# Moving one row of each partition to short transfers at the two ends of a DMA-fed softmax

## The chip, the core and the metric

The kernel runs on one core of a Trainium2 chip. The metric is the device time of one execution in microseconds (us): the median of several runs. A profile is one further execution with the hardware profiler on; its span runs from the first to the last instruction that it records.

## The reference

The input `logits` has the shape (2, 8, 2112, 2112) in float32, `rel_bias` (8, 33). For each batch, head and query row the kernel adds a bias that depends on the clipped distance of query and key, and takes a softmax over the 2112 keys:

```python
rel = pos[:, None] - pos[None, :]
bias = rel_bias[:, np.clip(rel, -16, 16) + 16]
logits = logits + bias[None]
e = np.exp(logits - logits.max(axis=-1, keepdims=True))
out = e / e.sum(axis=-1, keepdims=True)
```

So 285 MB are read, 285 MB are written, and each row of 2112 numbers (8448 bytes) is worked on by itself.

## The kernel before

There are 2 x 8 x 2112 rows. Each of the 128 partitions owns 264 consecutive ones (`ROWS`), so partitions 0 to 63 hold the first batch and 64 to 127 the second. A tile is 6 rows of every partition (`R`), one contiguous stretch of 50,688 bytes per partition in memory, 6.5 MB in all. Four buffers `X[0]` to `X[3]` hold tiles; 44 tiles go through them in turn, and each is changed in place and stored from where it was loaded.

**SP issues every large DMA.** First the 6 rows of tile 0 by one DMA each (line 88), then tiles 1 to 3 whole (line 78). Then it stores tile 0 (line 82, called from line 203) and enters its loop (lines 204 to 208). There, for each buffer in turn, it waits until the next tile has been scaled, issues that tile's store, waits until the store of the buffer before has landed (`st[b]`), and issues the load of a new tile into that buffer. After the loop come the stores of the last three tiles, the very last in two halves of 3 rows, and the waits for the stores. An instruction of SP that waits holds up all that SP would issue after it.

**ACT** issues one small DMA for `rel_bias` (line 97) and afterwards computes: for each row an exponential with its sum (line 175). **DVE** builds the table `M` of biases in PSUM (lines 118 to 155). Then it loops over 11 steps of 24 rows: `strip` copies the piece of `M` that this step needs into `F` (line 160); `add` waits for a buffer's load (`ld[b]`), and adds bias and finds the row maximum, one instruction per row (line 166); `scale` takes reciprocals of the sums (line 183) and multiplies the rows (line 187), three at a time. DVE works in program order: the six adds of a tile, then its six multiplications. **POOL** makes two small index tables (lines 101, 102) and is idle from then on.

The order of all this is written out by hand, with semaphores: `pre` and `ld` for loads, `st` for stores, `added`, `expd`, `inv` and `scaled` between DVE, ACT and SP. `take` waits for a semaphore and lowers it again. The waits appear in the profile under line 74.

Of the kernel before, what the change touches and what calls it, by code (L numbers as in the profile page):

```python
# [7 lines left out]
FP32 = mybir.dt.float32  # L8
I32 = mybir.dt.int32
EXP = mybir.ActivationFunctionType.Exp  # L10
ALU = mybir.AluOpType
# [4 lines left out]
def kernel(  # L16
# [21 lines left out]
    MW = S + ROWS - 1  # L38
    FW = S + STEP - 1
    BIG = 3.0e38  # L40

    io = ctx.enter_context(tc.tile_pool(name="io", bufs=1))
# [6 lines left out]
    ip = io.tile([P, 3, PB], I32, tag="ip", name="ip")  # L49
    ps = ctx.enter_context(tc.tile_pool(name="ps", bufs=1, space=bass.MemoryType.PSUM))  # L50
    M = ps.tile([P, 4096], FP32, tag="M", name="M")

    def view(t, offset, dims):

        return bass.AP(tensor=t.tensor, offset=t.offset + offset, ap=[[list(t.ap[0])[0], P]] + dims)

    def rows(t, j, n):

        return bass.AP(tensor=t.tensor, offset=t.offset + j * S, ap=[[ROWS * S, P], [1, n * S]])

    with tc.tile_critical(no_gpsimd_drain=True):
        ld = [nc.alloc_semaphore(f"ld{b}") for b in range(NBUF)]
# [8 lines left out]
        dve = nc.alloc_semaphore("dve")  # L71

        def take(eng, sem, n):
            eng.wait_ge(sem, n).then_inc(sem, -n)  # L74

        def load(j, b):
            nc.sync.dma_start(out=X[b][:, :], in_=rows(logits, j, R)).then_inc(ld[b], 16)

        def store(j, b, s0=0, n=R):  # L80
            take(nc.sync, scaled, n)
            nc.sync.dma_start(
                out=rows(out, j + s0, n), in_=X[b][:, s0 * S : (s0 + n) * S]
            ).then_inc(st[b], 16)

        for r in range(R):
            nc.sync.dma_start(
                out=X[0][:, r * S : (r + 1) * S], in_=rows(logits, r, 1)
            ).then_inc(ld[0] if r == R - 1 else pre, 16)  # L90
        for n in range(1, NBUF):
            load(n * R, n)

# [8 lines left out]
        nc.gpsimd.iota(ip[:, 2], pattern=[[1, PB]], base=0, channel_multiplier=0).then_inc(idx, 1)  # L102

        v = nc.vector
        done = [0]
# [5 lines left out]
        def settle():  # L111
# [7 lines left out]
                             op0=ALU.logical_shift_right, op1=ALU.bitwise_and))  # L119
# [7 lines left out]
        for m, op in ((eq, ALU.is_equal), (gt, ALU.is_gt), (le, ALU.is_le), (lt, ALU.is_lt)):  # L127
# [4 lines left out]
            out=view(F, 0, [[W, H], [1, W]]), in0=view(F, 0, [[W, H], [1, W]]),  # L132
            in1=view(F, SC + 3 * PB, [[1, H], [0, W]]), op=ALU.mult))
# [8 lines left out]
            out=view(F, 0, [[W, PB], [1, W]]), in0=view(F, SC + 2 * PB, [[1, PB], [0, W]]),  # L142
            in1=view(rbS, W - 1, [[0, PB], [-1, W]]), op=ALU.mult))
# [6 lines left out]
            out=view(M, U, [[ROWS, PB], [1, W]]), in0=view(F, 0, [[W, PB], [1, W]]),  # L150
            in1=view(F, SC + 8 * PB, [[1, PB], [0, W]]), op=ALU.add))
        then(v.tensor_copy(out=view(M, U + W, [[ROWS, PB], [1, ROWS - W]]),  # L152
                           in_=view(F, SC + 7 * PB, [[1, PB], [0, ROWS - W]])))
# [4 lines left out]
        def strip(j):  # L158

            v.tensor_copy(out=F[:, :], in_=M[:, bass.ds(ROWS - STEP - j, FW)]).then_inc(dve, 1)  # L160

        def add(b):
            take(v, ld[b], 16)
            for r in range(b * R, (b + 1) * R):
                x = X[b][:, (r - b * R) * S : (r - b * R + 1) * S]
                v.tensor_tensor_reduce(  # L166
                    out=x, in0=x, in1=F[:, STEP - 1 - r : STEP - 1 - r + S], scale=-1.0, scalar=BIG,
                    op0=ALU.add, op1=ALU.min, accum_out=nmax[:, r : r + 1],
                ).then_inc(added, 1)

        def exps(b):
            for r in range(b * R, (b + 1) * R):
                x = X[b][:, (r - b * R) * S : (r - b * R + 1) * S]
                take(nc.scalar, added, 1)
                nc.scalar.activation(  # L175
                    out=x, in_=x, func=EXP, scale=-1.0, bias=nmax[:, r : r + 1],
                    accum_out=tot[:, r : r + 1],
                ).then_inc(expd, 1)

        def scale(b):  # L180
            for r0 in range(b * R, (b + 1) * R, HALF):
                take(v, expd, HALF)
                v.reciprocal(out=rec[:, r0 : r0 + HALF], in_=tot[:, r0 : r0 + HALF]).then_inc(inv, 1)  # L183
                take(v, inv, 1)
                for r in range(r0, r0 + HALF):
                    x = X[b][:, (r - b * R) * S : (r - b * R + 1) * S]
                    v.tensor_scalar_mul(out=x, in0=x, scalar1=rec[:, r : r + 1]).then_inc(scaled, 1)  # L187

        v.sem_inc(dve, -done[0])
        take(v, pre, 16 * (R - 1))  # L190
        with nc.Fori(0, ROWS - STEP + 1, STEP, engines=[ENG.DVE]) as j:  # L191
            strip(j)
            take(v, dve, 1)
            for b in range(NBUF):
                add(b)
                scale(b)
        with nc.Fori(0, ROWS // STEP, 1, engines=[ENG.Activation]):
# [14 lines left out]
        store((N - 1) * R, (N - 1) % NBUF, HALF, R - HALF)  # L212
        for b in range(NBUF):
            take(nc.sync, st[b], 32 if b == (N - 1) % NBUF else 16)

# [28 lines left out]
```

## Time and profile before

| | us |
|---|---|
| median of 3 runs | 1331.23 |
| lowest, highest run | 1330.0, 1331.38 |
| span of the profiled execution | 1327.7 |
| median less span (what lies around the span) | 3.5 |
| DVE busy | 976.6 |
| ACT busy | 575.2 |
| POOL busy | 0.4 |

For the profiled execution the span is what is known of its time, so the 3.5 us between it and the median are taken for what lies around a span. The profile also records the packets of the core's 16 DMA engines: when each started, how long it took, how many bytes it carried, and on which queue. SP's DMAs are queue q1, ACT's are q10. A packet's engine number isn't recorded. In tables of windows the DMA share and the rate count a packet where it starts, so in windows of a few us a share can pass 1.

### The profile page before, as it was taken

To read this page: it belongs to the slowest core of one execution; us is meant where nothing else is said; L and a number is where in the kernel's file an instruction comes from. 1 tells how busy PE (TensorE), PEld (TensorE's weight loads), DVE (VectorE), ACT (ScalarE), POOL (GpSimd) and SP (SyncE) were. 2 spreads that over 40 slices of the span, in tenths; PEclk is the share of its full clock that TensorE was granted. 3 is DMA by queue.
4 is the path that set the end of the run, shared out by engine and by line. 5 is a ranking of instruction groups with operands and counts; after the bars stand their busy time and mean duration, and the time that the engine had idled before them with its cause. 6 is when DMAs were issued, how large, how long until landed. Compare 5 with 4: busy or idle time off the path is not lost. (4 is left out here: it accounts for less than half of the span.)

```text
span 1327.7 us, 2454 instructions
## 1 busy us (share of the span) xinstructions
DVE 976.6 (74%) x911; ACT 575.2 (43%) x539; POOL 0.4 (0%) x6
## 2 busy tenths in 40 slices
DVE  6999667777777776687778777677877776687772
ACT  2564333444444343345444333444444343335440
POOL 0000000000000000000000000000000000000000
DMA  9999999999999999999999999999999999999998
GB/s 392 431 428 437 435 420 437 435 434 425 435 437 434 428 435 434 435 429 429 438 438 432 426 438 437 437 425 437 437 437 425 435 440 437 428 432 438 437 426 359
DMA packets 13683, 571.11 MB, mean 430 GB/s; under 512 B 1521, under 2 KB 1649, under 8 KB 1649
## 3 DMA queue, kind: packets, MB, share of 16 engines
q1 hardware_dynamic: 13536, 570.96, 99.6%
q10 hardware_dynamic: 144, 0.14, 0.1%
q14 instruction: 3, 0.02, 0.0%
HBM read 285.61 MB, written 285.47 MB: 430 GB/s over the span
## 5 line engine op out<-in xcount | busy, mean ns | idle before, releaser
L166 DVE CUSTOM_DVE_ANT_0 X<-X,F 128x2112 f32<-128x2112 f32 x264 | 605.2, 2354 | 301.3 <-DVEq L74 301.3
L175 ACT ACTIVATE X<-X,nmax 128x2112 f32<-128x2112 f32 x264 | 541.7, 2052 | 539.3 <-ACTq L74 517.6
L187 DVE TENSOR_SCALAR X<-X,rec 128x2112 f32<-128x2112 f32 x264 | 332.4, 1315 | 13.2
L175 ACT ACT_TABLE_LOAD x11 | 14.1, 1283 | 183.3 <-ACTq L74 183.3
L175 ACT ACTIVATION_READ_ACCUMULATOR X<-X,nmax 128x1 f32 x264 | 49.2, 186 | 0.0
L160 DVE COPY F<-M 128x2135 f32 x11 | 26.1, 2374 | 6.3 <-DVEq L74 6.3
L166 DVE DVE_READ_ACCUMULATOR2_ANT nmax<- 128x1 f32 x264 | 21.7, 82 | 0.0
L183 DVE RECIPROCAL rec<-tot 128x3 f32<-128x3 f32 x88 | 14.9, 170 | 0.0
L131 DVE TENSOR_TENSOR F<-F 128x264 f32<-128x264 f32 x1 | 0.4, 434 | 4.7 <-DMA F<-in_rel_bias_dram 4.7
L152 DVE COPY M<-F 128x1848 f32<-128x1848 f32 x1 | 2.1, 2077 | 0.0
L118 DVE TENSOR_SCALAR ip<-ip 128x8 int32<-128x8 int32 x1 | 0.2, 173 | 1.3 <-POOL ip L102 1.3
L135 DVE TENSOR_REDUCE rbS<-F 128x33 f32<-128x264 f32 x1 | 0.6, 610 | 0.0
L149 DVE TENSOR_TENSOR M<-F 128x264 f32<-128x264 f32 x1 | 0.4, 441 | 0.0
L141 DVE TENSOR_TENSOR F<-F,rbS 128x264 f32<-128x264 f32 x1 | 0.4, 425 | 0.0
L128 DVE TENSOR_SCALAR F<-F 128x8 f32<-128x8 f32 x4 | 0.4, 166 | 0.0
L154 DVE COPY M<-rbS 128x247 f32<-128x247 f32 x1 | 0.4, 408 | 0.0
L139 DVE TENSOR_SCALAR F<-F,rbS 128x8 f32<-128x8 f32 x1 | 0.2, 231 | 0.0
L145 DVE SCALAR_TENSOR_TENSOR F<-F,rbS 128x8 f32<-128x8 f32 x1 | 0.2, 225 | 0.0
L140 DVE TENSOR_SCALAR F<-F,rbS 128x8 f32<-128x8 f32 x1 | 0.2, 222 | 0.0
L146 DVE SCALAR_TENSOR_TENSOR F<-F,rbS 128x8 f32<-128x8 f32 x1 | 0.2, 219 | 0.0
L124 DVE TENSOR_TENSOR F<-ip 128x8 f32<-128x8 int32 x1 | 0.2, 167 | 0.0
L121 DVE TENSOR_TENSOR F<-ip 128x8 f32<-128x8 int32 x1 | 0.2, 166 | 0.0
(9 smaller groups left out, 1.2 us busy)
## 6 DMA issues: line engine op xcount, KB each, us to landing
X<-in_logits_dram SPq DMA_DIRECT2D x43, 6336.0 KB, 44.6
out_dram<-X SPq DMA_DIRECT2D x43, 6336.0 KB, 52.6
X<-in_logits_dram SPq DMA_DIRECT2D x6, 1056.0 KB, 12.1
out_dram<-X SPq DMA_DIRECT2D x2, 3168.0 KB, 21.1
F<-in_rel_bias_dram ACTq DMA_DIRECT2D x1, 132.0 KB, 6.2
```

Source lines behind the costliest of these rows:

```text
L128: then(v.tensor_scalar(out=m, in0=dp, scalar1=0.0, scalar2=None, op0=op))
L131: then(v.tensor_tensor(out=view(F, 0, [[W, H], [1, W]]), in0=view(F, 0, [[W, H], [1, W]]), in1=view(F, SC + 3 * PB, [[1, H], [0, W]]), op= ...
L135: then(v.tensor_reduce(out=rbS[:, :], in_=view(F, 0, [[1, W], [W, H]]), axis=mybir.AxisListType.X, op=ALU.add))
L141: then(v.tensor_tensor(out=view(F, 0, [[W, PB], [1, W]]), in0=view(F, SC + 2 * PB, [[1, PB], [0, W]]), in1=view(rbS, W - 1, [[0, PB], [-1, ...
L149: then(v.tensor_tensor(out=view(M, U, [[ROWS, PB], [1, W]]), in0=view(F, 0, [[W, PB], [1, W]]), in1=view(F, SC + 8 * PB, [[1, PB], [0, W]] ...
L152: then(v.tensor_copy(out=view(M, U + W, [[ROWS, PB], [1, ROWS - W]]), in_=view(F, SC + 7 * PB, [[1, PB], [0, ROWS - W]])))
L154: then(v.tensor_copy(out=M[:, 0:U], in_=low.to_broadcast([P, U])))
L160: v.tensor_copy(out=F[:, :], in_=M[:, bass.ds(ROWS - STEP - j, FW)]).then_inc(dve, 1)
L166: v.tensor_tensor_reduce(out=x, in0=x, in1=F[:, STEP - 1 - r : STEP - 1 - r + S], scale=-1.0, scalar=BIG, op0=ALU.add, op1=ALU.min, accum_ ...
L175: nc.scalar.activation(out=x, in_=x, func=EXP, scale=-1.0, bias=nmax[:, r : r + 1], accum_out=tot[:, r : r + 1],).then_inc(expd, 1)
L183: v.reciprocal(out=rec[:, r0 : r0 + HALF], in_=tot[:, r0 : r0 + HALF]).then_inc(inv, 1)
L187: v.tensor_scalar_mul(out=x, in0=x, scalar1=rec[:, r : r + 1]).then_inc(scaled, 1)
```

## The change

One row (number 5, `XR`) of each partition leaves the tiles. In tile 0, SP loads and stores rows 0 to 4 alone. The rest goes by transfers of 8 partitions each, eight of them for 64 partitions (`few` names the 8 rows in memory, `fewx` the place in `X[0]`; the 8 partitions of a transfer lie 4 apart):

- **Row 5 of partitions 64 to 127** is loaded and stored by POOL. POOL clears row 5 of the lower 64 partitions in `X[0]`, resets the cursor by which its transfers choose DMA engines, and issues eight pairs: a transfer of 8 single numbers into the scratch tile `pad` (`skip`, meant to take up engines 0 to 7), and 8 rows of logits (meant for engines 8 to 15). It then waits for `told`, and issues eight such pairs again, this time with 8 rows stored to `out`. Semaphore `hx[i]` counts the eight row transfers, `sk[i]` the skips.
- **DVE** waits ahead of its loop for the clearing and for all eight `hx`, and computes all six rows of tile 0 as before (in the lower half of row 5, on zeros that are never stored).
- **SP** stores rows 0 to 4 of tile 0, raises `told`, and waits until all eight `hx` show 32, that is, until POOL's stores have landed. Only then it enters its loop.
- **Row 5 of partitions 0 to 63** is loaded after SP's loop into row 0 of `X[0]`, by eight DMAs of SP, once the last store from `X[0]` has landed. DVE, ACT and DVE work on it after the last tile (add, exponential, reciprocal, multiplication on 64 partitions), and SP stores it by eight DMAs, its last.

```diff
-        for r in range(R):
+        def few(t, half, i, r):
+            p = half * HP + (i // 4) * 32 + i % 4
+            return bass.AP(tensor=t.tensor, offset=t.offset + (p * ROWS + r) * S, ap=[[4 * ROWS * S, 8], [1, S]])
...
+        def skip(i, c):
+            w = list(pad.ap[0])[0]
+            nc.gpsimd.dma_start(
+                out=bass.AP(tensor=pad.tensor, offset=pad.offset + c, ap=[[w, 8], [1, 1]]),
+                in_=bass.AP(tensor=rel_bias.tensor, offset=rel_bias.offset, ap=[[W, 8], [1, 1]]),
+            ).then_inc(sk[i], 16)
+
+        for r in range(XR):
             nc.sync.dma_start(
                 out=X[0][:, r * S : (r + 1) * S], in_=rows(logits, r, 1)
-            ).then_inc(ld[0] if r == R - 1 else pre, 16)
+            ).then_inc(ld[0] if r == XR - 1 else pre, 16)
...
+        g = nc.gpsimd
+        g.memset(X[0][0:HP, XR * S : R * S], 0.0).then_inc(zero, 1)
+        g.inc_swdge_sem([], values=[], queue_num=0, mode="reset_dge_cursor")
+        for i in range(EX):
+            skip(i, i)
+            g.dma_start(out=fewx(1, i, XR), in_=few(logits, 1, i, XR)).then_inc(hx[i], 16)
+        g.wait_ge(told, 1)
+        for i in range(EX):
+            g.wait_ge(sk[i], 16)
+            g.wait_ge(hx[i], 16)
+            skip(i, EX + i)
+            g.dma_start(out=few(out, 1, i, XR), in_=fewx(1, i, XR)).then_inc(hx[i], 16)
...
-        take(v, pre, 16 * (R - 1))
+        take(v, pre, 16 * (XR - 1))
+        v.wait_ge(zero, 1)
+        for i in range(EX):
+            v.wait_ge(hx[i], 16)
         with nc.Fori(0, ROWS - STEP + 1, STEP, engines=[ENG.DVE]) as j:
...
+        xx = X[0][0:HP, 0:S]
+        take(v, xl, 16 * EX)
+        v.tensor_tensor_reduce(out=xx, in0=xx, in1=M[0:HP, ROWS - 1 - XR : ROWS - 1 - XR + S], ...)
+        take(v, expd, 1)
+        v.reciprocal(out=rec[0:HP, 0:1], in_=tot[0:HP, 0:1]).then_inc(inv, 1)
+        take(v, inv, 1)
+        v.tensor_scalar_mul(out=xx, in0=xx, scalar1=rec[0:HP, 0:1]).then_inc(scaled, 1)
...
-        store(0, 0)
+        take(nc.sync, scaled, R)
+        nc.sync.dma_start(out=rows(out, 0, XR), in_=X[0][:, 0 : XR * S]).then_inc(st[0], 16)
+        nc.sync.sem_inc(told, 1)
+        for i in range(EX):
+            nc.sync.wait_ge(hx[i], 32)
         with nc.Fori(0, ROWS - 2 * STEP + 1, STEP, engines=[ENG.SP]) as j:
...
+        take(nc.sync, st[0], 16)
+        for i in range(EX):
+            nc.sync.dma_start(out=fewx(0, i, 0), in_=few(logits, 0, i, XR)).then_inc(xl, 16)
         for n in range(N - NBUF + 1, N - 1):
             store(n * R, n % NBUF)
...
+        take(nc.sync, scaled, 1)
+        for i in range(EX):
+            nc.sync.dma_start(out=few(out, 0, i, XR), in_=fewx(0, i, 0)).then_inc(xs, 16)
```

More of the change, by code (lines that the diff above doesn't have):

```diff
@@ L40 @@
     BIG = 3.0e38
+    XR = R - 1
+    HP = P // 2
+    EX = 8
     io = ctx.enter_context(tc.tile_pool(name="io", bufs=1))
@@ L49 @@
     ip = io.tile([P, 3, PB], I32, tag="ip", name="ip")
+    pad = io.tile([P, 2 * EX], FP32, tag="pad", name="pad")
     ps = ctx.enter_context(tc.tile_pool(name="ps", bufs=1, space=bass.MemoryType.PSUM))
@@ L71 @@
         dve = nc.alloc_semaphore("dve")
+        zero = nc.alloc_semaphore("zero")
+        told = nc.alloc_semaphore("told")
+        xl = nc.alloc_semaphore("xl")
+        xs = nc.alloc_semaphore("xs")
+        hx = [nc.alloc_semaphore(f"hx{i}") for i in range(EX)]
+        sk = [nc.alloc_semaphore(f"sk{i}") for i in range(EX)]
         def take(eng, sem, n):
@@ L84, in store, with fewx @@
             ).then_inc(st[b], 16)
-        for r in range(R):
+        def few(t, half, i, r):
+            p = half * HP + (i // 4) * 32 + i % 4
+            return bass.AP(
+                tensor=t.tensor, offset=t.offset + (p * ROWS + r) * S, ap=[[4 * ROWS * S, 8], [1, S]]
+            )
+        def fewx(half, i, r):
+            p = half * HP + (i // 4) * 32 + i % 4
+            w = list(X[0].ap[0])[0]
+            return bass.AP(
+                tensor=X[0].tensor, offset=X[0].offset + p * w + r * S, ap=[[4 * w, 8], [1, S]]
+            )
+        def skip(i, c):
[5 more added lines that the diff above has]
+        for r in range(XR):
             nc.sync.dma_start(
                 out=X[0][:, r * S : (r + 1) * S], in_=rows(logits, r, 1)
-            ).then_inc(ld[0] if r == R - 1 else pre, 16)
+            ).then_inc(ld[0] if r == XR - 1 else pre, 16)
         for n in range(1, NBUF):
@@ L102 @@
         nc.gpsimd.iota(ip[:, 2], pattern=[[1, PB]], base=0, channel_multiplier=0).then_inc(idx, 1)
+        g = nc.gpsimd
[11 more added lines that the diff above has]
+        for i in range(EX):
+            g.wait_ge(sk[i], 32)
+            g.wait_ge(hx[i], 32)
         v = nc.vector
@@ L196 @@
                 scale(b)
+        xx = X[0][0:HP, 0:S]
+        take(v, xl, 16 * EX)
+        v.tensor_tensor_reduce(
+            out=xx, in0=xx, in1=M[0:HP, ROWS - 1 - XR : ROWS - 1 - XR + S], scale=-1.0, scalar=BIG,
+            op0=ALU.add, op1=ALU.min, accum_out=nmax[0:HP, 0:1],
+        ).then_inc(added, 1)
+        take(v, expd, 1)
+        v.reciprocal(out=rec[0:HP, 0:1], in_=tot[0:HP, 0:1]).then_inc(inv, 1)
+        take(v, inv, 1)
+        v.tensor_scalar_mul(out=xx, in0=xx, scalar1=rec[0:HP, 0:1]).then_inc(scaled, 1)
         with nc.Fori(0, ROWS // STEP, 1, engines=[ENG.Activation]):
@@ L199 @@
                 exps(b)
-        store(0, 0)
+        take(nc.scalar, added, 1)
+        nc.scalar.activation(
+            out=xx, in_=xx, func=EXP, scale=-1.0, bias=nmax[0:HP, 0:1], accum_out=tot[0:HP, 0:1],
+        ).then_inc(expd, 1)
+        take(nc.sync, scaled, R)
[3 more added lines that the diff above has]
+            nc.sync.wait_ge(hx[i], 32)
         with nc.Fori(0, ROWS - 2 * STEP + 1, STEP, engines=[ENG.SP]) as j:
@@ L212 @@
         store((N - 1) * R, (N - 1) % NBUF, HALF, R - HALF)
-        for b in range(NBUF):
+        take(nc.sync, scaled, 1)
+        for i in range(EX):
+            nc.sync.dma_start(out=few(out, 0, i, XR), in_=fewx(0, i, 0)).then_inc(xs, 16)
+        take(nc.sync, xs, 16 * EX)
+        for b in range(1, NBUF):
             take(nc.sync, st[b], 32 if b == (N - 1) % NBUF else 16)
```

## The prediction

> **What bounds the kernel now.** I read the page's shares and slices first, then the DMA queues, then the two ends.
>
> ```profile
> span 1327.7 us, 2454 instructions
> DVE 976.6 (74%) x911; ACT 575.2 (43%) x539; POOL 0.4 (0%) x6
> DMA  9999999999999999999999999999999999999998
> q1 hardware_dynamic: 13536, 570.96, 99.6%
> q10 hardware_dynamic: 144, 0.14, 0.1%
> ```
>
> DMA is the bound: 16 engines busy in every slice, almost all with SP's queue q1, while DVE has a quarter of the span free. SP's 94 DMAs make 13536 packets, 144 each: 128 of data (one per partition) and 16 that report the end, so nine per engine. The rate is the first price; the tail shows what is left to gain.
>
> ```profile
> 80.00:319.20 239.20, 182.64 (x168) 105.19 (x100) 0.00 (x0) 1.00 1.00 432
> 1036.80:1276.00 239.20, 176.52 (x162) 104.58 (x98) 0.00 (x0) 1.00 1.00 434
> ...
> 1318.00:1320.00 2.00, 0.00 (x0) 0.00 (x0) 0.00 (x0) 1.00 1.09 469
> 1320.00:1321.00 1.00, 0.00 (x0) 0.00 (x0) 0.00 (x0) 1.00 0.53 228
> 1321.00:1322.00 1.00, 0.00 (x0) 0.00 (x0) 0.00 (x0) 1.00 0.47 203
> 1322.00:1323.00 1.00, 0.00 (x0) 0.00 (x0) 0.00 (x0) 1.00 0.41 177
> 1323.00:1324.00 1.00, 0.00 (x0) 0.00 (x0) 0.00 (x0) 1.00 0.41 177
> 1324.00:1325.00 1.00, 0.00 (x0) 0.00 (x0) 0.00 (x0) 1.00 0.18 76
> 1325.00:1326.00 1.00, 0.00 (x0) 0.00 (x0) 0.00 (x0) 1.00 0.12 51
> ```
>
> The last column is GB/s. At 434 each engine moves 27.1; a row of 8448 bytes takes 0.312 us, a tile's packet of 50,688 bytes 1.87, a row of all partitions (eight per engine) 2.49, a tile 14.95. In the tail 177 GB/s are seven packets of 25,344 bytes a microsecond: nine engines are done at about 1321, seven go on to 1326.2 (the last packet of 0.94 us starts before 1326). They carry equal bytes, so seven have fallen some 5 us behind. Early in the run the rate is 432, later 434: on average an engine loses 0.5% of 239 us there, 1.1 us, so I read the lag as losses early in the run (engines disturbing each other while in step), none once they stand apart. Were all to end together near 1321, up to 5 us could be had, 0.4%. Which engines lag the trace doesn't tell.
>
> **The change, part by part.** The bytes of every engine stay. If the transfers go where the change says, engines 8 to 15 do a row's load and store (2 x 2.49 = 5.0 us) first, which engines 0 to 7 do last. This puts the halves 5.0 us apart from the start, as the seven laggards end up, and takes it back at the end. Alone that is worth the 5 us. What it costs is decided in the first 80 us.
>
> ```profile
> 2.00:4.00 2.00, 0.43 (x5) 0.00 (x0) 0.00 (x0) 1.00 0.87 168
> 4.00:6.00 2.00, 0.00 (x0) 0.00 (x0) 0.00 (x0) 1.00 0.87 280
> 6.00:8.00 2.00, 0.81 (x2) 0.00 (x0) 0.00 (x0) 1.00 0.96 396
> ...
> 0.92 0.41 ACTq L97 DMA_DIRECT2D F<-in_rel_bias_dram  x1
> 0.97 3.34 SPq L88 DMA_DIRECT2D X<-in_logits_dram  x6
> 43.07 22.23 SPq L82 DMA_DIRECT2D out_dram<-X  x2
> 81.12 0.36 SPq L78 DMA_DIRECT2D X<-in_logits_dram  x1
> ...
> F<-in_rel_bias_dram ACTq DMA_DIRECT2D x1, 132.0 KB, 6.2
> ```
>
> *When the engines run dry.* The queue starts at 2 us (1.1 after the issue); the three windows fall short of 434 by 0.53, 0.31 and 0.08 MB, 2.1 us. Four tiles loaded and one stored are 30 rows, 74.7 us. So the first store has left at about 79; SP sees it landed at 81.1. The second store was issued at 65.0 (43.07 and 22.23 later less the issue), 14 us before it was needed. After the change engines 8 to 15 still have work until 79, engines 0 to 7, short of two rows, until 74.2. The second store must be issued 1.1 us before that.
>
> *The new wait in SP.* The second store now stands behind the landing of POOL's eight stores, issued only after `told`, with the first store. Queued behind it in SP: all later stores and loads. What do POOL's transfers cost on engines full of SP's packets? The nearest row is ACT's small DMA: 132 KB, 0.3 us of data, needs 6.2 us to land, 5.1 after the queue starts. That fits nine packets per engine, each after one of SP's 0.31 us rows: the queues take turns, a packet each (nine turns: 2.8 us, the rest the slow start). Behind tile packets a turn costs 1.87. Eight pairs have at least one packet of each transfer on each engine they report from, 16 turns, or 24 where data and report go separately: 30 to 45 us. From 43 (no delay of tile 0) this ends at 73 to 88; but at 74 and 79 SP's packets are used up and the rest goes at once. I take 79 plus landing (81.1 - 79, 2 us): SP goes on at about 80.5, the second store moves at 81.6. Engines 0 to 7 stand still for 7 us, 8 to 15 for 2.5, and **both restart together**: the 5 us of distance is gone.
>
> By the Trainium skill ("DMA: Bandwidth & Descriptors", section "Why a DMA increments its semaphore by 16 and not by 1") a transfer issued by GpSimd reports from all 16 engines, whatever its shape. By that the turns are paid on engines 0 to 7 too; no run before the change has such a transfer. Without it only engines 8 to 15 would pay, and the sum, which ends at 79 on these, stays.
>
> *DVE's start.*
>
> ```profile
> 1.13 0.14 POOL L102 IOTA ip<- 128x8 int32 x1
> ...
> 9.75 2.08 DVE L152 COPY M<-F 128x1848 f32<-128x1848 f32 x1
> 18.48 2.38 DVE L160 COPY F<-M 128x2135 f32 x1 [6.26 <-DVEq L74]
> 21.17 2.36 DVE L166 CUSTOM_DVE_ANT_0 X<-X,F 128x2112 f32<-128x2112 f32 x1 [0.31 <-DVEq L74]
> ```
>
> POOL clears 2112 columns (0.14 us by its own small rows, 2.4 by DVE's copy, taken: done at 3.7), resets the cursor (taken at 0.1 to 1), then issues 16 transfers. An issue is bounded by 0.35 (SP's) and, no POOL transfer being traced, some 2 us; I take 0.9, nearer 1.1, from issue to first packet at the queue's start, than SP's. They are out at 18.5; up to about 15.5 turns cost 0.31, then 1.87, so the last two or three pairs land at 25 to 33. `strip` now comes after this wait instead of beside the last load: first add at 28 to 36 instead of 21.2. The first store then goes out at 50 to 58 (21.9 after the add), before engines 0 to 7 have loaded all (74.2 - 12.5 = 61.7): no pause. The second tile is scaled at 72 to 80, as late as POOL's stores land: the two delays lie side by side. `told` is later too, but the engines still drain at 79. From about 1.1 us an issue on, the last POOL store is itself later than that.
>
> *The rest.* Eight more packets each way per engine and some 30 reports: 0.3 us. The extra DMA issues at SP's end:
>
> ```profile
> L78 SPq DMA_DIRECT2D X<-in_logits_dram x43: 349/349/664, 4.4 to 1237.1; - x43
> L175 ACT ACTIVATE X<-X,nmax 128x2112 f32<-128x2112 f32 x264 | 541.7, 2052 | 539.3 <-ACTq L74 517.6
> 1237.05 0.35 SPq L78 DMA_DIRECT2D X<-in_logits_dram  x1
> 1243.89 60.13 SPq L82 DMA_DIRECT2D out_dram<-X  x4
> 1281.81 2.36 DVE L166 CUSTOM_DVE_ANT_0 X<-X,F 128x2112 f32<-128x2112 f32 x1 [8.06 <-DVEq L74]
> 1299.82 3.78 DVE L187 TENSOR_SCALAR X<-X,rec 128x2112 f32<-128x2112 f32 x3
> ```
>
> SP waits for `st[0]` until about 1267 (one tile before 1281.8), then issues eight short loads (3 to 5 us) ahead of the store that went out at 1243.9; the last tile's load keeps the engines busy until 1282, so it is hidden. DVE's extra add, the exponential and the multiplication (2.4 + 2.2 + 1.5 us) end at 1310, its eight stores are out by 1314; the engines have work until 1321. Hidden by 7 us; without that cover some 6 us.
>
> **The sum.** Both halves restart at 81.6 instead of going on at 79: +2.5. In step again, seven engines fall behind by 5 as before. If these are of 8 to 15: 1326.2 + 2.5 + 0.3 = 1329.0. Engines 0 to 7 have the two rows still to do: 1321 + 2.5 + 5.0 + 0.3 = 1328.8. The end comes 2.8 later: span 1330.5, with the 3.5 around it **1334.0 us**.
>
> **The rivals.**
> - *POOL's stores land before 74* (quick issues, few turns): no pause, the distance stays, all engines end near 1321.3: span 1322.8, 1326.3 us. At 75 to 77, part of it: 1327 to 1330. For: the engines' gap of 5 us is real, and the seven lose nothing more once apart. Against: 16 turns of 1.87 in 31 us leave no room.
> - *The laggards are of engines 0 to 7* (slower): after the joint restart they end at 1326.2 + 2.5 + 5.0 + 0.3 = 1334.0, 1339.0 us. It decides once the second store starts both halves together. The trace names no engine; nine to seven says little.
> - *POOL issues slowly* (slower): at 1.5 us a transfer, 16 loads are out at 28, land near 45, `told` comes at 70, and 16 more issues end at 94, some 14 us after 80: 1348. At 1.3, half of it. Also if DVE's multiplications hold POOL up: two groups of 3.78 per tile, 7.6 us.
>   The Trainium skill ("SBUF — State Buffer", section "A bandwidth-pool intuition that's wrong (but worth ruling out)" with the box ahead of it) says that descriptors of GpSimd's DMAs can't be written while DVE runs in a mode that takes two ports; 620 ns alone became 3100. The trace of before has no transfer of POOL to show it.
> - *The cursor isn't where the change wants it* and POOL's rows run on engines 0 to 7: these carry four rows more at the two ends than the others, 5 us over the sum: 1339. Or they spread over all 16: no distance arises, and 1334 stays.
>   The same DMA page, section "Rules for kernel authors", says not to bother with transfers to two partition halves, since both spray over all engines; no row here shows a transfer of eight partitions.
>
> **How the numbers follow.** The forecast (1331 to 1337, by when the restart comes, 80 to 83): 34%, about half of it beyond 1333.9. Early stores: 30%, of which 26 under 1328.6. Laggards in the lower half: 14%. Slow POOL: 15%. Cursor: 7%. A measurement of this kernel can tell 0.2% (2.7 us) from no change. Faster 0.26, same 0.20, slower 0.54. The range leaves out the best end of the early stores and the worst of slow POOL: 1326.5 to 1345.
>
> **What would show it.** SP's second store: issued at 80 to 82 with an idle gap on the engines just before (rate far under 434 between 74 and 82) is my step; by 73 is the first rival. POOL's own issue times and the landing of its stores show the turns. DVE's first add at 28 to 36. In the tail: full rate to the last 2 us means that the distance held; half of the engines working alone for 5 us means it did not. I am wrong at the root if small transfers don't wait a turn per packet, or if engines in step no longer fall behind.

## The result and the profile after

The changed kernel takes **1348.36 us** (median of 4 runs, 1347.14 to 1350.65), the kernel before, measured beside it, 1331.31 (4 runs, 1330.0 to 1332.12): a ratio of **1.013, interval 1.0116 to 1.0144**. It is slower by 17 us; 1334.0 was forecast, and 1345 was the upper end of the range. The two profiled spans differ by 19.0 us (1346.7 and 1327.7), and the accounts below are of these. The 2 us more are of the kernel before: each run of the changed kernel took 1.7 to 1.8 us more than its own span, while the median of before is 3.5 above the span that was profiled, so that execution was some 1.7 faster than the median one.

The page of the changed kernel, as the page of before was read: span, rate by slice, queues.

```profile
span 1346.7 us, 2541 instructions
GB/s 337 434 357 410 434 434 434 431 434 434 431 434 434 434 434 432 432 432 434 434 434 434 434 432 435 431 435 434 435 434 435 434 432 435 432 435 432 438 423 266
q1 hardware_dynamic: 13648, 569.87, 98.4%
q0 software_dynamic: 1024, 1.08, 0.3%
```

Still bound by DMA, at the same 434 GB/s in the middle. The time is lost at both ends: a slice is 33.7 us, so the first and third (337, 357) cover 0 to 34 and 67 to 101 us, the last (266) the tail. POOL's queue q0 carries almost nothing, 1.08 MB in 1024 packets, 32 for each of its 32 transfers.

**The start.** POOL's instructions and then SP's in order of time (start, length, engine, line, what), and what SP waited for in line 269 (total, times, longest):

```profile
10.80 0.52 POOL L139 DMA_DIRECT2D X<-in_logits_dram  x1
49.30 0.52 POOL L112 DMA_DIRECT2D pad<-in_rel_bias_dram  x1 [37.99 <-SPq L267]
...
56.94 0.52 POOL L145 DMA_DIRECT2D out_dram<-X  x1
```

```profile
48.62 0.34 SPq L266 DMA_DIRECT2D out_dram<-X  x1
85.42 0.36 SPq L92 DMA_DIRECT2D out_dram<-X  x1
86.06 0.37 SPq L88 DMA_DIRECT2D X<-in_logits_dram  x1
92.17 0.34 SPq L92 DMA_DIRECT2D out_dram<-X  x1
```

```profile
SPq L269 <- DMA out_dram<-X: 35.8, 4, 34.8
```

POOL issues quickly, 0.52 us a transfer: its loads are out at 11.3, its stores at 57.5. But SP, which waits for these stores from 49 on, goes on at 85.42, 20 us after the 65.0 of before. Windows of both kernels (length, busy engines, clock, DMA share, GB/s), changed kernel first:

```profile
8.00:16.00 8.00, 4.33 (x10) 0.00 (x0) 3.31 (x7) 1.00 1.03 335
16.00:22.00 6.00, 0.00 (x0) 0.00 (x0) 0.00 (x0) 1.00 1.08 338
...
76.00:80.00 4.00, 4.00 (x5) 3.74 (x5) 0.00 (x0) 1.00 0.69 287
80.00:84.00 4.00, 3.99 (x5) 3.76 (x4) 0.00 (x0) 1.00 0.37 152
84.00:88.00 4.00, 3.86 (x4) 2.15 (x2) 0.00 (x0) 1.00 0.48 203
```

```profile
8.00:16.00 8.00, 4.12 (x10) 0.00 (x0) 0.00 (x0) 1.00 1.02 429
16.00:22.00 6.00, 3.21 (x2) 0.00 (x0) 0.00 (x0) 1.00 1.20 513
...
76.00:80.00 4.00, 3.85 (x7) 3.73 (x4) 0.00 (x0) 1.00 1.06 456
80.00:84.00 4.00, 3.85 (x5) 0.61 (x2) 0.00 (x0) 1.00 0.97 418
```

Two losses stand here. From 8 to 22 us the engines are as busy as before (share over 1) and move less: 94 GB/s less for 8 us and 175 for 6 are 1.8 MB, 4.1 us at 434. That counts a packet where it starts; the first engines to run dry say the same, at 78.3 in the table below where 74.2 was worked out for engines short of two rows. Row packets take longer: in the packet records the median of a row of SP's is 367 ns instead of 319, of a row of POOL's 396. From 76 on the engines fall idle, one group after the other, until SP's second store comes.

The packet records hold the 4-byte packets with which each engine reports the end of a transfer. Those of one large transfer make a group of 16; its first and last time tell how far the engines stand apart:

```
                      before            after
tile 3 loaded         64.3 to  65.5     65.8 to  69.8
first store out       79.2 to  80.4     78.3 to  83.2
second store out      94.2 to  95.4    101.8 to 102.4
the next load        109.2 to 110.8    118.0 to 118.8
around 1270 (change) 1260.8 to 1266.4  1269.7 to 1278.8
last packets         1320.6 to 1326.2  1330.9 to 1342.0
```

After the change the engines stood up to 4.9 us apart at 78 to 83, in two groups of eight (78.3 to 79.3 and 81.6 to 83.2), and 0.6 at 102: they restarted together, 7.6 us late, and one tile later 8.8. The packet records name where the last 1.7 us of this went. SP's second store started at 86.3, 7.1 after 79.2, where the first store of before was out. Of its eight packets on each engine the last took 2.50 us in the median instead of 1.87, and of the load behind it the last took 3.09, on all 16 engines: 0.5 and 1.2 us. Why, no run shows. Around 1270 the first engines are still 8.9 behind those of before.

**The end.** SP's last instructions, the windows of the tail, and the DRAIN with which POOL ends the program (ns shortest/median/longest; the same row of before behind it):

```profile
1249.45 0.34 SPq L88 DMA_DIRECT2D X<-in_logits_dram  x1
1279.22 5.54 SPq L277 DMA_DIRECT2D X<-in_logits_dram  x8
1284.88 31.55 SPq L92 DMA_DIRECT2D out_dram<-X  x4
1322.42 9.71 SPq L284 DMA_DIRECT2D out_dram<-X  x8
```

```profile
1330.00:1331.00 1.00, 0.00 (x0) 0.00 (x0) 0.00 (x0) 1.00 0.95 406
1331.00:1332.00 1.00, 0.00 (x0) 0.00 (x0) 0.00 (x0) 1.00 0.59 253
...
1334.00:1337.00 3.00, 0.00 (x0) 0.00 (x0) 0.00 (x0) 1.00 0.40 166
1337.00:1338.00 1.00, 0.00 (x0) 0.00 (x0) 0.00 (x0) 1.00 0.18 76
1338.00:1342.00 4.00, 0.00 (x0) 0.00 (x0) 0.00 (x0) 1.00 0.06 23
```

```profile
L313 POOLq DRAIN  x3: 46/214/2674, 1342.8 to 1346.4; - x3
```

```profile
L240 POOLq DRAIN  x3: 34/41/64, 1326.8 to 1327.4; - x3
```

The first engines are done at 1330.9. Half of the engines carry the late rows: seven of these end at about 1334.7 to 1336.9, two engines without late rows at 1338.6, and from 1338.6 on one engine works alone, with eight late rows as its last packets, until 1342.0 (23 GB/s from 1338 to 1342, near the 27 of one engine). Then POOL drains for 2.7 us.

| what | us |
|---|---|
| both halves restart late, first engines (109.2 to 118.0) | 8.8 |
| the last engine's distance to the first ones around 1270: 6.4 for one straggler instead of 5.6 for the last | 0.8 |
| its late rows, load and store (16 x 0.312) | 5.0 |
| not assigned, on the same engine | 1.2 |
| last packet to the end of the span: 4.7 instead of 1.5 | 3.2 |
| sum | 19.0 |

The table follows the engine that ended last. Around 1270 three engines stood 6.4, 9.1 and 9.1 behind the first. Which of them has late rows is worked out: the first engines would end at 1329.4 (1320.6 + 8.8); 9.1 more is 1338.5, where the two without late rows end, and 6.4 + 5.0 more is 1340.8, for the one that ends at 1342.0.

### The profile page after: what moved, and what is told of

The parts are those of the page before. It is cut to its first block, busy times and chain, and to the rows that moved or that the text cites. A ratio compares the mean times of both kernels' runs of the same rounds, so it can differ in the third digit from the quotient of the medians.

```text
span 1346.7 us, 2541 instructions
## 1 busy us (share of the span) xinstructions
DVE 982.0 (73%) x915; ACT 577.3 (43%) x541; POOL 18.6 (1%) x39
## 3 DMA queue, kind: packets, MB, share of 16 engines
q0 software_dynamic: 1024, 1.08, 0.3%
## 5 line engine op out<-in xcount | busy, mean ns | idle before, releaser
L206 DVE COPY F<-M 128x2135 f32 x11 | 26.1, 2376 | 11.6 <-DMA X<-in_logits_dram 11.6
L112 POOL DMA_DIRECT2D pad<-in_rel_bias_dram x16 | 8.4, 526 | 38.0 <-SPq L267 38.0
L139 POOL DMA_DIRECT2D X<-in_logits_dram x8 | 4.1, 519 | 0.0
L145 POOL DMA_DIRECT2D out_dram<-X x8 | 4.1, 518 | 0.0
```

Of the source, the lines that this page charges most:

```text
L112: nc.gpsimd.dma_start(out=bass.AP(tensor=pad.tensor, offset=pad.offset + c, ap=[[w, 8], [1, 1]]), in_=bass.AP(tensor=rel_bias.tensor, offs ...
L139: g.dma_start(out=fewx(1, i, XR), in_=few(logits, 1, i, XR)).then_inc(hx[i], 16)
L145: g.dma_start(out=few(out, 1, i, XR), in_=fewx(1, i, XR)).then_inc(hx[i], 16)
```

## The experiments

Each was compared with the kernel before on the same chip (medians 1329.7 to 1330.0). The first theory was that of the prediction: SP's wait for POOL's stores stops the engines and destroys a distance that would have stopped the falling behind. Its rivals: the small transfers themselves cost the time; or the late rows do.

**1. The wait one store later.** Base: the changed kernel.

```diff
-        for i in range(EX):
-            nc.sync.wait_ge(hx[i], 32)
+        for n in range(NBUF):
+            store((n + 1) * R, (n + 1) % NBUF)
+            if n == 0:
+                for i in range(EX):
+                    nc.sync.wait_ge(hx[i], 32)
+            take(nc.sync, st[n], 16)
+            load((n + NBUF) * R, n)
...
```

> The changed kernel, with SP's wait for POOL's eight stores moved behind the store of tile 1 (it stays ahead of the load that reuses X[0]). Theory A (the loss comes from SP standing still behind this wait, and from the joint restart of the engines that follows, which wipes out the 5 us between the halves): the second store goes out when tile 1 is scaled, at about 71 us, no window between 70 and 95 falls under 350 GB/s, the halves stay 5 us apart, nobody falls behind further, and all engines end within 3 us of each other: time 1327 to 1332. Theory B (POOL's transfers cost the engines time by themselves, and the distance does nothing against falling behind): the pause goes, but engines still fall behind by 5 us, the two late rows come on top for engines 0 to 7: 1337 or more.

Measured: 1347.28, ratio 1.0134 [1.0117, 1.0151]. SP's instructions and two windows:

```profile
47.34 0.34 SPq L266 DMA_DIRECT2D out_dram<-X  x1
69.04 0.34 SPq L92 DMA_DIRECT2D out_dram<-X  x1
99.15 0.34 SPq L88 DMA_DIRECT2D X<-in_logits_dram  x1
```

```profile
92.00:96.00 4.00, 4.00 (x5) 2.83 (x3) 0.00 (x0) 1.00 0.55 232
96.00:100.00 4.00, 4.00 (x5) 3.74 (x5) 0.00 (x0) 1.00 0.08 32
```

The second store went out in time, at 69, and the pause moved to the next thing that POOL's stores held up, the load at 99.15. The engines were up to 5.4 us apart at 92.6 to 98.0, in two groups, and 1.3 at 116.9. With SP's queue full, eight pairs issued from about 48 to 56 landed near 98.5, after some 50 us or 27 packets of 1.87: the small transfers get a turn only when a whole packet of SP's ends. On an engine, the row of one pair starts 7.81 us after that of the pair before where SP sends tile packets: four turns of 1.87 and the row's 0.32. Where some of SP's packets were shorter, it is 5.9 to 6.6. No saving came from moving the wait.

**2. The same distance without POOL.** Base: before. Row 5 of tile 0 is loaded by 16 transfers of SP of 8 partitions each; the store stays whole.

```diff
+        def short(half):
+            for i in range(EX):
+                nc.sync.dma_start(out=fewx(half, i, XR), in_=few(logits, half, i, XR)).then_inc(hx, 16)
...
+            if r in (1, 3):
+                short(r // 2)
```

> The kernel before, with row 5 of tile 0 loaded by SP in 16 transfers of 8 partitions, for both halves, which should all run on engines 0 to 7; nothing of it goes back, and POOL issues nothing. Engines 0 to 7 get 2.5 us more to do, 8 to 15 2.5 us less: the halves are 5 us apart from the first load on. Theory A (engines in step fall behind, engines 5 us apart don't): 8 to 15 end near 1318.5, 0 to 7 near 1323.5, no stragglers, 2.7 us less than before: 1327.5 to 1329.5. Theory B (engines fall behind whatever the distance): stragglers 5 us later on top: 1333 to 1336.

Measured: 1334.36, 1.0034 [1.0022, 1.0047]. Two windows of the head and two of the tail:

```profile
8.00:14.00 6.00, 3.89 (x10) 0.00 (x0) 0.00 (x0) 1.00 1.01 425
14.00:22.00 8.00, 0.00 (x0) 0.00 (x0) 0.00 (x0) 1.00 1.05 283
1318.00:1322.00 4.00, 0.00 (x0) 0.00 (x0) 0.00 (x0) 1.00 1.00 431
...
1326.00:1331.00 5.00, 0.00 (x0) 0.00 (x0) 0.00 (x0) 1.00 0.06 25
```

Eight engines stand 3.1 to 4.4 us behind the first from the first tile on, and engines stop falling behind: beyond 72 us, the excess of slow tile packets (over 1890 ns) over 1872 ns is 2.7 us in all, against 29.5 before. 15 engines are done by 1326.6. But the head loses about 4 us (283 GB/s from 14 on, with no POOL transfer in the program), and one engine still creeps back, some 0.06 us in every transfer of 15 us (3.6 us behind the first at 96, 7.6 at 1173), and ends alone at 1330.9.

**3. POOL's small transfers alone.** Base: before, with 16 `skip` transfers of POOL at the start and a wait of POOL's for them.

```diff
+        for i in range(16):
+            nc.gpsimd.dma_start(out=bass.AP(tensor=pad.tensor, offset=pad.offset + i, ap=[[w, 8], [1, 1]]), ...).then_inc(sk, 16)
+        nc.gpsimd.wait_ge(sk, 16 * 16)
```

> The kernel before, with 16 transfers of 8 single numbers issued by POOL at the start, which nothing else waits for. Theory A (small packets of POOL's queue cost the engines some 0.1 us each in the head, and a kernel in which POOL has issued a DMA ends with POOL draining for 2.7 us): the rate in 8 to 16 us falls under 400 GB/s, 2 to 3 us are lost there, the end is 2.7 us later after the last packet: 1335 to 1338. Rival (tiny packets are free, the drain belongs to something else in the change): 1331.

Measured: 1331.72, 1.0013 [1.0003, 1.0022]. The head moves as before (419 and 522 GB/s from 8 to 16 and 16 to 22). The DRAIN:

```profile
L250 POOLq DRAIN  x3: 40/78/1357, 1328.1 to 1329.9; - x3
```

Tiny transfers cost the engines nothing that can be seen, and 1.36 us at the end: about 83 ns for each of POOL's transfers, 16 here, 32 and 2.67 us in the change.

**4. The change without POOL's queue.** Base: the changed kernel; the upper half of row 5 goes by one transfer of SP with 64 partitions each way.

```diff
+        nc.sync.dma_start(out=X[0][HP:P, XR * S : R * S], in_=up).then_inc(hx[0], 16)
...
-        for i in range(EX):
-            skip(i, i)
...
+        nc.sync.dma_start(out=upo, in_=X[0][HP:P, XR * S : R * S]).then_inc(hx[1], 16)
```

> The changed kernel without POOL's transfers: row 5 of the upper 64 partitions is loaded and stored by SP in one transfer of 64 partitions each way (four rows on each of the 16 engines), early and without a pause; the lower half goes last as in the change. Engines 0 to 7 have 5 us more to do than 8 to 15, and there is no distance until the end. If the laggards are engines of 8 to 15 alone, the end is at 1323.5 to 1325, time 1327 to 1330. If some engine of 0 to 7 lags by 5 us, it ends at 1328 to 1330, time 1333 to 1335. If short stores at the end are themselves slow to issue, SP's last issue stands later than the engines' last other packet, and more.

Measured: 1335.23, 1.0035 [1.002, 1.005]. No pause (426 GB/s from 72 to 96), no long drain, second store at 69.25; the last packet ends at 1330.9. The head is slow here too (297 GB/s from 16 to 22). Each against before as measured beside it, this version loses 5.5 us and the change 17.1: POOL's queue, with the wait for it, costs 11.6 of the 17. How the 5.5 part into the head and the late rows this run doesn't show.

**5. The distance made later.** Base: before; 16 transfers of SP with 8 partitions load row 5 of tile 3 instead of tile 0.

```diff
+        T = NBUF - 1
+        nc.sync.dma_start(out=X[T][:, 0 : XR * S], in_=rows(logits, T * R, XR)).then_inc(hx, 16)
+        for half in (1, 0):
+            for i in range(EX):
+                nc.sync.dma_start(out=fewx(half, i, XR, T), in_=few(logits, half, i, T * R + XR)).then_inc(hx, 16)
...
```

> The kernel before, with row 5 of tile 3 (not tile 0) loaded by SP in 16 transfers of 8 partitions on engines 0 to 7, issued behind the other loads, where nobody waits for them before 70 us; SP passes the report on to the load's own semaphore. No POOL transfer, nothing late. Engines 8 to 15 have 2.5 us less to do than before, 0 to 7 2.5 more; 5 us apart from about 65 us on. If engines that stand apart don't fall behind, 8 to 15 end near 1318.5, 0 to 7 near 1323.5, and the time is 2 to 3 us under before. If the slow head of the run with short transfers in tile 0 (4 us lost) comes from short transfers as such and not from DVE or SP waiting there, 2 to 4 us are lost here too, and it is no faster than before.

Measured: 1332.5, 1.0018 [1.0008, 1.0027]. The tail:

```profile
1314.00:1318.00 4.00, 0.00 (x0) 0.00 (x0) 0.00 (x0) 1.00 1.04 450
1318.00:1323.00 5.00, 0.00 (x0) 0.00 (x0) 0.00 (x0) 1.00 0.48 208
1323.00:1324.00 1.00, 0.00 (x0) 0.00 (x0) 0.00 (x0) 1.00 0.18 76
1324.00:1329.00 5.00, 0.00 (x0) 0.00 (x0) 0.00 (x0) 1.00 0.06 25
```

This is the clearest picture of the mechanism. Eight engines are done by 1318.8, seven by 1324.7, the 5 us that the rows put between them; slow packets add up to 2.7 us instead of 29.5, and the head loses nothing. One engine of the second half creeps at the pace of experiment 2: 5.8 us behind the first at 92, 10.0 at 1168, 11.1 when it ends at 1329.1, later than the last engine of before. That one engine eats the gain. It is also nearly all that is still lost: counted over every tile packet, not only those over 1890 ns, the excess is 5.3 us, about its own creep. And it is the two groups that must stand apart, not each engine from the next: the first eight keep within 0.8 us of one another all the way and lose nothing.

**6. Half of that distance's rows only.** Base: before; the lower half of tile 3's row 5 by one 64-partition transfer.

```diff
+        for i in range(EX):
+            nc.sync.dma_start(out=fewx(1, i, XR, T), in_=few(logits, 1, i, T * R + XR)).then_inc(hx, 16)
+        nc.sync.dma_start(out=X[T][0:HP, XR * S : R * S], in_=low).then_inc(hx, 16)
```

> As the run beside it, but with half of the distance: the lower half of row 5 of tile 3 goes by one transfer of 64 partitions over all 16 engines, the upper half by 8 short ones on engines 0 to 7, which get 1.25 us more to do and stand 2.5 us behind. If the distance must pass some 3 us to keep engines from falling behind (where the laggards of before came to rest, 3.2 to 5.6 us), some still fall behind, to 3 or 4 us: last end 1323 to 1325. If 2.5 is enough: 1322.3, time 4 us under before.

Measured: 1332.97, 1.002 [1.001, 1.003]. The second eight engines stand 3.6 to 4.9 us behind the first engine, only 1.6 behind the last of the first eight; slow packets add up to 2.4 us, all but one are done by 1325.3, and one creeps to 1329.1 again. A smaller distance holds as well and doesn't cure the one.

**7. POOL loads, SP stores.** Base: the changed kernel; the upper half of row 5 is stored by SP with 64 partitions, so SP never waits for POOL.

```diff
-        g.wait_ge(told, 1)
...
-            g.dma_start(out=few(out, 1, i, XR), in_=fewx(1, i, XR)).then_inc(hx[i], 16)
...
+        nc.sync.dma_start(out=upo, in_=X[0][HP:P, XR * S : R * S]).then_inc(up, 16)
```

> The changed kernel with POOL's loads, but without POOL's stores: the upper half of row 5 is stored by SP in one transfer of 64 partitions, nobody waits for POOL after the loads. The lower half goes late as in the change. If POOL's stores and SP's wait for them make the pause (theory A), no window from 70 to 120 us falls under 380 GB/s, and the second store goes out at 70; the slow head (4 us) stays, the late rows cost engines 0 to 7 up to 5 us, and POOL's drain is half: 1336 to 1341. If the pause stays, it isn't POOL's stores: 1347. Where POOL's rows run also shows here, since no common restart wipes it out: if they run on engines 8 to 15 as the change says, these are 2.5 us behind until the tail and ahead by 2.5 after it; if on engines 0 to 7, these end 7.5 us behind the others.

Measured: 1341.7, 1.0085 [1.0067, 1.0103]: 11.8 us over before, where the change is 17.1 over.

```profile
8.00:22.00 14.00, 4.00 (x10) 0.00 (x0) 3.31 (x7) 1.00 1.05 347
72.00:96.00 24.00, 23.70 (x23) 15.06 (x15) 0.00 (x0) 1.00 1.01 422
```

The pause is gone (422 GB/s), the slow head is still there (347). From 110 us on the engines are smeared over 3.1 us instead of standing in two groups, and they fall behind as after a joint restart: slow packets add up to 66.5 us (40.1 of it beyond 120 us, against 27.0 before), eight engines are 3.5 to 8 us late by 1200, and with the late rows on top the last ends at 1337.4. So a spread of 3 us without a gap protects nothing.

**8. Nothing late.** Base: the changed kernel; the lower half of row 5 is loaded and stored with tile 0 by 8 transfers of SP each way, POOL's part and SP's wait as in the change.

```diff
+        for i in range(EX):
+            nc.sync.dma_start(out=fewx(0, i, XR), in_=few(logits, 0, i, XR)).then_inc(xl, 16)
...
-            nc.sync.dma_start(out=fewx(0, i, 0), in_=few(logits, 0, i, XR)).then_inc(xl, 16)
...
```

> The changed kernel with its POOL transfers and SP's wait as they are, but without the late part: the lower half of row 5 is loaded and stored with tile 0, by 8 short transfers of SP each way, so that nothing is late and both halves have their full share early. If the late rows cost 5 us on engines 0 to 7 after the joint restart, and their issues 1.3 us before the last stores: time 1341 to 1344, the tail as in the kernel before (seven or so stragglers of 4 to 6 us). If the late rows are free: 1348.

Measured: 1346.5, 1.0122 [1.0104, 1.014]. SP's second store goes out at 89.42 and is out at 105.8, 4.0 later than in the change; the last packet ends at 1340.3. From the end of that store to the last packet are 1234.5 us here, 1240.2 with the late rows and 1232.0 before (94.2 to 1326.2). The late rows therefore cost 5.7 us of the change; what remains after a joint restart falls behind by 2.5 more than before, 1.1 of it in the slow load behind the second store (16.1 us where before took 15.0) and 1.4 in the last straggler (7.0 us behind the first around 1180 instead of 5.6).

**9. One engine of the eight spared.** Base: experiment 5; row 5 of tile 3 goes by 16 transfers of 7 partitions and one of 16.

```diff
+        for p in range(0, P, 8):
+            some(p, 1, 7)
+        some(7, 8, 16)
```

> As the run with 16 short transfers in tile 3, where 15 engines kept their distance and one of engines 0 to 7 crept 4.5 us further behind over the run. Here row 5 of tile 3 goes by 16 transfers of 7 partitions, meant for engines 0 to 6, and one of 16 partitions: engines 0 to 6 get 2.8 us more to do than before, engine 7 and engines 8 to 15 2.2 us less. If the creeping engine is number 7, it now has 5 us in hand, nobody ends after 1325, and the time is 1327 to 1329, a little under before. If it is one of 0 to 6, it ends near 1329.5 as in the other run: 1332.5 to 1333.

Measured: 1333.91, 1.0029 [1.0019, 1.0039]. Nine engines lead and seven lag, so a transfer of 7 partitions uses seven engines; the creeping engine is still among the laggards (ends 1330.4). If the seven are of the eight, it isn't the one that was spared.

**10 and 11. All short rows by POOL, in both orders of a pair.** Base: experiment 5; tile 3's row 5 by 16 pairs of POOL, `skip` then row as in the change, or row then `skip`.

```diff
+        for half in (1, 0):
+            for i in range(EX):
+                g.dma_start(out=bass.AP(tensor=pad.tensor, ...), ...).then_inc(sk, 16)
+                g.dma_start(out=fewx(half, i, XR, T), in_=few(logits, half, i, T * R + XR)).then_inc(rw, 16)
```

> The kernel before, with row 5 of tile 3 loaded by POOL in 16 pairs as the change writes them (8 single numbers, then 8 rows), so that, if the cursor works as the change says, engines 8 to 15 take all these rows and stand 5 us behind, 0 to 7 ahead; nobody waits for them before 65 us, POOL stores nothing. If so, the creeping engine, one of 0 to 7, is hidden in the 5 us, all end by 1325, POOL's drain adds 2.7: span 1329, time 1331 to 1333. If the rows run on engines 0 to 7, the creeping engine ends last, at 1329 as with SP's short transfers, plus the drain: span 1333.5, time 1335 to 1337.

> The run beside it with the order in each pair turned round: 8 rows first, then 8 single numbers. If the cursor works as the change says, the rows now go to engines 0 to 7, and the two runs trade places: the creeping engine ends last, span 1333.5, time 1335 to 1337, against 1331 to 1333 there. If the order makes no difference to the end, the pairs don't choose the engines in this way.

Measured: 1337.0, 1.0051 [1.0034, 1.0067], and 1337.69, 1.0052 [1.0035, 1.0069]. In both, eight engines stand ahead of eight others (first to first 4.5 to 4.8 us), and one of the laggards creeps to 1330.8 and 1332.1. All rows of POOL fall on the same eight engines; which eight, these two can't tell. Both heads are slow (333 and 315 GB/s from 8 to 16).

**12. Each half by its own queue.** Base: experiment 5; the upper half of tile 3's row 5 by 8 pairs of POOL in the change's order, the lower half by 8 transfers of SP. If POOL's rows run on engines 8 to 15, every engine gets eight rows and no distance arises; on the same eight as SP's, 16 rows against none put 5.0 us between the halves.

```diff
+        for i in range(EX):
+            nc.sync.dma_start(out=fewx(0, i, XR, T), in_=few(logits, 0, i, T * R + XR)).then_inc(hx, 16)
...
+        for half in (1,):
+            for i in range(EX):
+                g.dma_start(out=bass.AP(tensor=pad.tensor, ...), ...).then_inc(sk, 16)
+                g.dma_start(out=fewx(half, i, XR, T), in_=few(logits, half, i, T * R + XR)).then_inc(rw, 16)
```

> The kernel before, with row 5 of tile 3 in short transfers: the upper half by 8 pairs of POOL as the change writes them, the lower half by 8 short transfers of SP, which run on engines 0 to 7. If POOL's rows run on engines 8 to 15, every engine has its own eight rows, as in the kernel before: no distance between halves at 100 us (under 2 us), stragglers fall behind by 4 to 6 us as before, span about 1329 to 1331 with POOL's drain of 1.3. If POOL's rows run on engines 0 to 7 as well, these are 5 us behind from about 65 us on, with nothing else falling behind but the one creeping engine: span 1331 to 1333, and eight completions 5 us after the other eight at 100 us.

Measured: 1335.49, 1.0043 [1.0026, 1.006]. The tail:

```profile
1316.00:1320.00 4.00, 0.00 (x0) 0.00 (x0) 0.00 (x0) 1.00 0.97 418
1320.00:1325.00 5.00, 0.00 (x0) 0.00 (x0) 0.00 (x0) 1.00 0.61 264
1325.00:1326.00 1.00, 0.00 (x0) 0.00 (x0) 0.00 (x0) 1.00 0.24 101
1326.00:1330.00 4.00, 0.00 (x0) 0.00 (x0) 0.00 (x0) 1.00 0.06 25
```

The halves are 2.4 us apart once POOL's rows are in (37.2 to 39.8), and 5 us after SP's (eight reports from 79.6 to 80.5, eight from 84.5 to 85.7). The rows of POOL ran **on the same eight engines as SP's**. The change puts both its early and its late rows on one half.

## Why the prediction was wrong

The step that failed is the restart term of the sum: put at 2.5 us, it measured 8.8. Two more went wrong: the sum gave the late rows to engines that didn't lag, and it put POOL's end at nothing. Against the forecast span of 1330.5 the measured 1346.7 is 16.2 more: 6.3 of the restart, 6.7 of that engine (0.8 + 5.0 + 1.2 of the table, less the 0.3 that the sum had), 3.2 of the end.

- **Rate, bound, tail of before: right.** Engines in step lose, two groups apart don't; what it is that disturbs them, no run shows. Experiments 2, 5, 6 and 9 to 12, with a gap of 1.6 to 5.1 us between the last engine of one group and the first of the other, keep the excess of slow packets at 2.2 to 3.1 us against 29.5. "None once they stand apart" held for 15 engines; the sixteenth creeps whatever was tried, and takes back what the others gain. So the 5 us on which the first rival rested weren't to be had this way.
- **Turns: right in kind, too few.** Packet by packet, as argued. But a pair takes four turns, not the two or three of the prediction: in the change the rows of POOL's stores start 5.3 to 7.8 us apart on an engine, and half of them (32 of 64) were still waiting when SP's packets ran out; those went between 81.6 and 84.2. The sum had a way out of this, that the rest goes at once, and it held. By the Trainium skill ("DMA: Bandwidth & Descriptors", section "Why a DMA increments its semaphore by 16 and not by 1") all 16 engines report for such a transfer; the trace agrees as far as it goes: each has 32 packets, 8 with rows and 24 of 4 bytes, and 137 of the 4-byte ones go between 78.2 and 79.5, when the leading eight engines run dry, while the rows wait for the others until 81.6.
- **POOL's issue: too dear.** 0.52 us, where I took 0.9 and a rival 1.5. The loads were in earlier, and the first add came at 26.73, ahead of the 28 to 36 forecast. The third rival (slow issues) is out. Its other form, multiplications that hold POOL up, wasn't tried: from 49.3 to 57.5 DVE ran adds only.
- **"Both halves restart at 81.6 instead of going on at 79: +2.5": this term failed in size.** The mechanism came as written, SP's second store as the gate and the distance wiped out; the size was 8.8. SP went on at 85.4, not 80.5. The head lost about 4 us, which nothing in the trace of before showed and the sum put at nothing; that moves the 79 to 83, and the last of POOL's rows went until 84.2. The store then ended 7.6 us late, 0.5 of it in its last packets, and 1.2 more were lost in the last packets of the following load. Experiment 7 bears out the gate: without POOL's stores the pause is gone.
- **"Engines 8 to 15 do a row first, which engines 0 to 7 do last": false** (experiment 12). The prediction followed the change's own words and gave the cursor 7%. It cost the change no time by itself: after a joint restart only the late rows still count, so the rival's 5 us over the sum fell away with the distance. The same section of the Trainium skill has both readings, a cursor from which consecutive engines are taken in turn, and an exception for some direct copies, in which GpSimd's transfer is spread over all 16 engines, each with a sixteenth of the partitions, rounded up. Worked out from that, 8 partitions would fill the first eight. Experiment 12 agrees with the exception and not with the cursor, as far as records without engine numbers can: the rows ran on the same eight as SP's.
- **"If these are of 8 to 15": false for one engine.** Of the three that fell furthest behind after the restart, two have no late rows and end at 1338.6, one has them and ends at 1342.0. That is the second rival's mechanism (1339.0 us), the one on the slower side, with the larger restart term on top. Experiment 8 gives the late rows' price, 5.7 us, against the 5.0 worked out there.
- **"Hidden by 7 us": nearly right.** The eight short loads do hold back the next store, from about 1279 to 1284.88, and the first engines, dry at 1284.6, lose some 1.3 us there; but the engine that ends last had work throughout, so the end didn't move by it. The eight short stores were issued from 1322.42 to 1332.13, not out by 1314, and the first engines ended at 1330.9: hardly any of the 7 us of cover was left.
- **What lies around: missed.** POOL's DRAIN, 2.67 us, isn't in any step of mine; with it the end stands 3.2 further from the last packet. The 3.5 us added to the span held some 1.7 that lie around no span: the profiled execution of before was a fast one.

Still open: why row packets slow down in the head when tile 0's row is split or POOL moves rows beside it, and stay at 319 ns with tiny transfers (3) or short rows behind whole tiles (5, 6, 9). In the change their median in windows of 2 us is 346 to 515 ns from 8 us on, and experiments 1, 7, 8 and 10 to 12 are slow there too (315 to 349 GB/s from 8 to 16); in 2 and 4 the last rows are the slowest (medians of 660 and 717 from 18 to 20). Open as well: why the last packets behind the restart are slow, and what holds one engine back. No version that was run beats the kernel before.

## What to carry to other kernels

Before crediting a plan that places transfers on chosen DMA engines, test the placement alone: give one half by each of two ways and see whether a distance appears. A small transfer on a second queue waits one whole packet of the main queue per turn, so with packets of 1.87 us, and four turns for each pair, a wait on eight pairs of them costs some 50 us; nothing that feeds the main queue should stand behind such a wait. A gain that is the mean of 16 engines is worth only what the last of them lets through: look at each engine's end, not at the mean.

## What the runs showed of the hardware

- Each transfer that POOL issues adds about 83 ns to POOL's DRAIN at the end of the program: 1.36 us for 16 (experiments 3, 7, 12), 2.67 for 32 (the change, 1, 8, 10, 11).
- Two groups of engines with a gap of 1.6 to 5.1 us between them hardly disturb one another (2.2 to 3.1 us of slow packets in the run), though the engines of a group can be within 0.8 us of each other. Where all 16 stood without such a gap early in the run or after the restart it is 29.5 before, 34.0 and 38.7 in experiments 3 and 4, and 65 to 67 in the change and in experiments 1, 7 and 8; of these last, 24 to 32 fall from 90 to 120 us, mostly in the last packets of two transfers of SP.
- A transfer of 8 partitions ran on the same eight engines whether SP or POOL issued it (experiment 12: 2.4 us between the groups after POOL's rows, 5 after SP's).
- SP's issue of eight short stores took 9.71 us in the tail of the change, 1.2 each, and 5.40 to 6.53 in experiments 1, 4 and 8; of eight short loads 5.54, 0.69 each; against 0.35 for a whole tile.
